# A forward pass on one core: the attention heads divide their outputs instead of their weights, and run in a fixed order on TensorE

## The chip, the core and the metric

The kernel runs on one core of a Trainium2 chip. The core has a matrix engine (TensorE, PE in the profile; its weight loads are listed apart as PEld), VectorE (DVE), ScalarE (ACT), GpSimd (POOL) and SyncE (SP), which here issues the loads from memory. The engines share an on-chip memory (SBUF) and the accumulators that TensorE writes into (PSUM), and run side by side, joined by semaphores. The metric is the time of one execution in microseconds, as the median of several runs: 2803.64 us for the kernel before (three runs, 2803.21 to 2806.1).

## The reference, cut to what matters

A sequence of 512 positions with 1024 features goes through two layers with four mixing branches each ("mix") and two feed-forward blocks, then a recurrent block, an MLP, a banded attention with 16 heads, and another MLP. Two places have heads: the latent attention of each mix (8 heads), and the banded attention. Both end in a softmax and a product with the values:

```python
# in each mix, per block of 128 queries q0:kend, for 8 heads
s = (einsum('bqhd,bkhd->bhqk', q_nope[:, q0:kend], k_nope[:, :kend])
     + einsum('bqhr,bkr->bhqk', q_rope[:, q0:kend], k_rope[:, :kend])) * scale
p = jax.nn.softmax(where(mask, s, NEG_INF), axis=-1)
outs.append(einsum('bhqk,bkhd->bqhd', p, v[:, :kend]))

# in the banded attention, per chunk of 64 queries, for 16 heads
sc = einsum('bqhd,bhkd->bhqk', qb, kb) * scale + bias
p = jax.nn.softmax(where(valid, sc, -inf), axis=-1)
o = einsum('bhqk,bhkd->bqhd', p, vb)
```

A softmax is an exponential divided by the sum of its row. The division can be done on the weights p, or, since the product is linear, on the rows of the output.

## The kernel before

All of it is float32. Activations lie transposed, as 8 tiles of 128 features by 512 positions. A large product is done as three matmuls of a shorter format (`mm3`, L149 to L153): high x high, high x low and low x high parts. The parts are made by `split` (L104): ScalarE copies the high part (L109), VectorE or GpSimd subtracts it for the low part (L110). `load` (L123) fetches weights and splits them; a gain is multiplied in on GpSimd (L138).

`heads` (L332) runs both kinds of heads. A head has four blocks of 128 queries, with 128, 256, 384 and 512 keys. `scores` (L270) makes a block's scores in one of two banks "s": TensorE's products (L279, or `mm3` in a mix), VectorE's row maximum (L291, or L295 with the bias), ScalarE's exponential with the row's sum beside it (L292, L297), VectorE's reciprocal of the sum (L298), and the scaling of the weights (L302 on VectorE for the first three blocks, L300 on ScalarE for the last). Two blocks later, `turn` (L305) transposes the scaled block on TensorE (L314) into one of two banks "t" and splits it into `pth` and `ptl`; after the fourth block, eight matmuls with the values follow (L325, "the products") into the only bank "o". ScalarE copies one half of that bank (L329), and `done` adds the other half to it on VectorE (L523 in a mix, L1030 in the attention).

In the attention a head's keys and queries come from `doubled` (L945): VectorE makes a tile `two` (L949), TensorE transposes it in four pieces (L953) into a bank "t". `stacked` (L957) splits the keys (`kh`, `kl`), and makes the queries `q` on ScalarE (L963) and VectorE (L965). All that is the step `prep`, done while the head before is at its second block.

What fills TensorE between the pieces of a head is `filler` (L1036): the projections of the next four heads' queries, keys and values (`quarter`, 256-wide matmuls), and then the first products of the attention's output. `heads` takes 96 such steps, spread evenly. A mix takes 68 steps of its other branches. The list `marks`, used in the attention alone, makes a step of the filler wait in the program's order for the turn before it. Everything else in the order of each engine is set by a scheduler, which takes instructions by priority when what they need is there by its own reckoning; the pieces of a head have a higher priority (`hi`) than the rest.

Of the kernel before, what the change touches and what calls it, by code (L numbers as in the profile page):

```python
# [18 lines left out]
P = 128  # L19
# [47 lines left out]
class Net:  # L67
    def __init__(self, ctx, tc, d, out):
# [6 lines left out]
        self.half = self.small.tile([P, 32], F32, name="half")  # L75
# [194 lines left out]
    def scores(self, it, qb):  # L270
# [5 lines left out]
        if rows is None:  # L276

            for a, n in zip(k, range(2)):
                nc.tensor.matmul(out=s[:, :w], lhsT=q[:, qs], rhs=a[:, :w], start=n == 0, stop=n == 1)  # L279
        else:  # L280
            self.mm3(s[:, :w], (q[0][rows, qs], q[1][rows, qs]), (k[0][rows, :w], k[1][rows, :w]), True, True)
# [7 lines left out]
        sm = self.t(self.small, "sm", 6, (P, 1))  # L289
# [8 lines left out]
        nc.vector.reciprocal(out=sm, in_=sm)  # L298
        if qb == 3:
            nc.scalar.activation(out=p, in_=p, func=AF.Copy, scale=sm)  # L300
        else:
            nc.vector.tensor_scalar(out=p[:, :w], in0=p[:, :w], scalar1=sm, scalar2=None, op0=ALU.mult)  # L302
        return p

    def turn(self, it, qb, p):  # L305
# [13 lines left out]
        if qb == 3:  # L319

            o = self.ps("o")
            for kb in range(4):
                bs = slice(4 * kb, 4 * kb + 4 - kb)
                for pt in (pth, ptl):
                    nc.tensor.matmul(out=o[:, kb * P:], lhsT=it["v"](kb), rhs=pt[:, bs],  # L325
                                     start=kb == 0 and pt is pth, stop=kb == 3 and pt is ptl)
# [3 lines left out]
            it["done"](o[a], f[a], a)  # L330

    def heads(self, items, filler, total, marks=None, hi=1000, depth=2):  # L332


        pend = []
        places, place, given = 8 * len(items) + 2 * depth, 0, 0

        def turn():
            with self.tc.high_priority(offset=hi):
                self.turn(*pend.pop(0))  # L340
            if marks is not None:
                marks.append(self.mark.ins)

        def fill():
            nonlocal place, given
            place += 1
            while given * places < total * place:
                given += 1
                with self.tc.issue_after(marks[-1]) if marks else ExitStack():
                    next(filler, None)  # L350

        items[0]["prep"](items[0])
        for n, it in enumerate(items):
            for qb in range(4):
                with self.tc.high_priority(offset=hi):
                    pend.append((it, qb, self.scores(it, qb)))
                fill()
                if len(pend) > depth:
                    turn()
                if qb == 1 and n + 1 < len(items):  # L360
                    items[n + 1]["prep"](items[n + 1])
                fill()
        while pend:
            fill()
            turn()
# [5 lines left out]
    def mix(self, l, gnext):  # L371
# [10 lines left out]
        with tc.tile_pool(name=f"att{l}", bufs=1, reuse_waits="tile") as ap:  # L382
# [136 lines left out]
            def item(hd):  # L519
                j = hd // 2  # L520

                def done(o, f, rows):
# [689 lines left out]
```

## Time and profile before

| | kernel before |
|---|---|
| median of 3 runs | 2803.64 us (2803.21 to 2806.1) |
| the profiled execution | 2796.84 us |
| its span, mean granted clock of TensorE | 2795.1 us, 0.991 |
| TensorE busy | 2719.6 us, 97%, 13616 matmuls |
| VectorE busy | 1570.9 us, 56% |
| ScalarE busy | 1148.8 us, 41% |
| GpSimd busy | 443.4 us, 16% |

The profiled execution is a run of its own; its span runs from the first to the last instruction. Busy times of different engines overlap, so they do not add up to the span. A granted clock of 1 is TensorE's higher level (2.4 GHz), 0.5 the lower (1.2 GHz). By the timeline, the first mix's heads run from about 78 to 199 us, the second's from about 890 to 1014, and the attention's from about 2196 to 2429.

### The profile page before, as it was taken

What the parts mean: (1) busy time and instruction counts of PE and PEld (TensorE: products, weight loads), DVE (VectorE), ACT (ScalarE), POOL (GpSimd) and SP (SyncE); (2) the same over time, 40 slices, a digit from 0 to 9 for tenths busy, and PEclk for the clock granted to TensorE, in tenths of its full rate; (3) what the DMA queues carried; (4) which work ended last, traced back from release to release, by engine and by line L of the source; (5) the groups of instructions that cost most, each with busy time, mean ns of one, the idle gap of its engine ahead of it and who ended that gap; (6) DMA issues with size and microseconds to landing.
All of it is one profiled execution on the core that took longest, in us unless ns stands there. A gap on an engine that the chain in (4) does not pass through costs nothing.

```text
span 2795.1 us, 34599 instructions
## 1 busy us (share of the span) xinstructions
PE 2719.6 (97%) x13616; PEld 2304.5 (82%) x13616; DVE 1570.9 (56%) x2420; ACT 1148.8 (41%) x1894; POOL 443.4 (16%) x350
## 2 busy tenths in 40 slices
PE   8999999999999999999999998999999999899999
PEld 7778889888898778888888886888888888788887
DVE  5875555534467865456344478744444688744443
ACT  5553234322255543234222358433323567533222
POOL 5401110100004211101000100100004674200000
PEclk9999999999999999999999999999999999999999
DMA  4213232233322123242333322233223211133322
GB/s 152 63 46 98 92 106 89 91 100 96 96 89 95 48 64 98 93 132 64 95 96 100 92 93 78 77 106 97 94 96 97 72 63 63 63 98 92 105 95 87
DMA packets 77348, 249.70 MB, mean 89 GB/s; under 512 B 8577, under 2 KB 14593, under 8 KB 77185
## 3 DMA queue, kind: packets, MB, share of 16 engines
q1 hardware_dynamic: 77184, 247.49, 27.7%
q8 instruction: 107, 1.75, 0.3%
q14 instruction: 57, 0.46, 0.1%
HBM read 245.36 MB, written 2.10 MB: 89 GB/s over the span
## 4 chain that ended last, share of the span: by engine, by line
PE 88%; DVE 7%; ACT 3%; issue 1%; DMA 0%; POOL 0%; SPq 0%; DVEq 0%; ACTq 0%
PE ps_mm L151 16%; PE ps_mm L152 16%; PE ps_mm L153 16%; PE ps_s L152 9%; PE ps_s L151 9%; PE ps_s L153 9%; PE ps_o L153 3%; PE ps_o L152 3%; PE ps_o L151 3%; PE ps_o L325 1%; PE ps_t L314 1%; PE ps_s L279 1%; DVE xl L237 1%; ACT wh L109 1%; DVE S L214 0%
## 5 line engine op out<-in xcount | busy, mean ns | idle before, releaser
L109 ACT ACTIVATE wh<-raw 128x1024 fp32r<-128x1024 f32 (+3 forms) x403 | 411.8, 1024 | 1178.8 <-PE ps_mm L152 458.0
L110 DVE TENSOR_TENSOR wl<-raw,wh 128x1024 fp32r<-128x1024 f32 (+3 forms) x403 | 514.8, 1279 | 164.8 <-ACT wh L109 155.0
L151 PE MATMUL ps_mm<-xh,wh 128*128 128x512 f32 x1160 | 453.8, 392 | 7.3 <-ACT xh L112 6.8
L152 PE MATMUL ps_mm<-xl,wh 128*128 128x512 f32 x1160 | 453.2, 391 | 0.5 <-DVE xl L113 0.5
L153 PE MATMUL ps_mm<-xh,wl 128*128 128x512 f32 x1160 | 452.7, 391 | 0.0
L151 PEld LDWEIGHTS ps_mm<-xh,wh 128*128 128x128 f32 x1160 | 218.4, 188 | 53.8 <-ACT xh L112 6.8
L152 PEld LDWEIGHTS ps_mm<-xl,wh 128*128 128x128 f32 x1160 | 218.5, 188 | 45.4 <-DVE xl L113 1.0
L153 PEld LDWEIGHTS ps_mm<-xh,wl 128*128 128x128 f32 x1160 | 218.3, 188 | 45.4
L153 PE MATMUL ps_s<-xh,wl 128*128 128x512 f32 x552 | 215.5, 390 | 0.0
L151 PE MATMUL ps_s<-xh,wh 128*128 128x512 f32 x552 | 215.1, 390 | 0.0
L152 PE MATMUL ps_s<-xl,wh 128*128 128x512 f32 x552 | 214.8, 389 | 0.0
L151 PE MATMUL ps_mm<-hh,wh 128*128 128x512 f32 (+1 forms) x422 | 161.2, 382 | 0.0
L152 PE MATMUL ps_mm<-hl,wh 128*128 128x512 f32 (+1 forms) x422 | 160.9, 382 | 0.0
L153 PE MATMUL ps_mm<-hh,wl 128*128 128x512 f32 (+1 forms) x422 | 160.9, 382 | 0.0
L690 POOL TENSOR_TENSOR a<-a,rb 128x512 f32<-128x512 f32 x44 | 60.2, 1371 | 534.2 <-DVE a L689 534.2
L624 POOL TENSOR_TENSOR m<-m,g 128x512 f32<-128x512 f32 x48 | 62.6, 1304 | 433.4 <-DVE g L623 433.3
L153 PEld LDWEIGHTS ps_s<-xh,wl 128*128 128x128 f32 x552 | 103.6, 188 | 22.3 <-DVE wl L110 0.9
L151 PEld LDWEIGHTS ps_s<-xh,wh 128*128 128x128 f32 x552 | 103.7, 188 | 21.4
L152 PEld LDWEIGHTS ps_s<-xl,wh 128*128 128x128 f32 x552 | 103.6, 188 | 21.4
L151 PE MATMUL ps_s<-hh,wh 128*128 128x512 f32 (+1 forms) x308 | 117.0, 380 | 0.0
L152 PE MATMUL ps_s<-hl,wh 128*128 128x512 f32 (+1 forms) x308 | 116.8, 379 | 0.0
L153 PE MATMUL ps_s<-hh,wl 128*128 128x512 f32 (+1 forms) x308 | 116.8, 379 | 0.0
(462 smaller groups left out, 5858.4 us busy)
## 6 DMA issues: line engine op xcount, KB each, us to landing
raw<-in_w_in SPq DMA_DIRECT2D x96, 512.0 KB, 3.5
raw<-in_w_gu SPq DMA_DIRECT2D x88, 512.0 KB, 3.5
raw<-in_w_down SPq DMA_DIRECT2D x80, 512.0 KB, 3.5
raw<-in_w_up SPq DMA_DIRECT2D x64, 512.0 KB, 3.5
raw<-in_w_down SPq DMA_DIRECT2D x32, 448.0 KB, 3.3
raw<-in_w_qkv SPq DMA_DIRECT2D x24, 512.0 KB, 3.4
raw<-in_w_out SPq DMA_DIRECT2D x16, 512.0 KB, 3.5
raw<-in_a_w_in SPq DMA_DIRECT2D x16, 512.0 KB, 3.6
```

The source lines that it names most:

```text
L109: a = nc.scalar.activation(out=h, in_=src, func=AF.Copy)
L110: b = (eng or nc.vector).tensor_tensor(out=l, in0=src, in1=h.bitcast(F32), op=ALU.subtract)
L151: mm(out=ps, lhsT=a[0], rhs=b[0], start=first, stop=False)
L152: mm(out=ps, lhsT=a[0], rhs=b[1], start=False, stop=False)
L153: self.multiplied = mm(out=ps, lhsT=a[1], rhs=b[0], start=False, stop=last)
L237: lambda: self.nc.vector.scalar_tensor_tensor(out=l, in0=x, scalar=g, in1=h.bitcast(F32), op0=ALU.mult, op1=ALU.subtract))
L279: nc.tensor.matmul(out=s[:, :w], lhsT=q[:, qs], rhs=a[:, :w], start=n == 0, stop=n == 1)
L314: self.mark = nc.tensor.transpose(out=pt[:, ks], in_=p[:, ks], identity=self.c("ident"))
L325: nc.tensor.matmul(out=o[:, kb * P:], lhsT=it["v"](kb), rhs=pt[:, bs], start=kb == 0 and pt is pth, stop=kb == 3 and pt is ptl)
L624: G.tensor_tensor(out=m, in0=m, in1=g, op=ALU.add)
L690: G.tensor_tensor(out=a, in0=a, in1=rb, op=ALU.mult)
```

## The change

The scaling of the weights and the reciprocals of single blocks go. The sums of a head's four blocks stand in one tile of four columns. After the products, VectorE takes one reciprocal of the four, TensorE spreads them over the partitions by four transposes (`spread`, L203) into a bank "t", and `done` gets a multiplication by that bank behind the addition. This holds for mixes and attention.

In the attention every piece is now tied to the one before (`behind`), so that TensorE's order there is written out and not left to the scheduler. The products follow a step of filler later than the last turn; keys' and queries' transposes go into the bank "o" in place of "t", and they and their tiles `two` are made at other places in the sequence, up to two heads ahead (`plan`). The filler has 88 steps in a pace of its own; the values of the first four heads (`lead`) are made between the first heads' transposes, and the keys of the second four before the heads. The widening of `half` has no use in these stages.

```diff
 def scores(self, it, qb):
...
-        sm = self.t(self.small, "sm", 6, (P, 1))
+        if qb == 0:
+            it["sm"] = self.t(self.small, "sm", 2, (P, 4))
+        sm = it["sm"][:, qb:qb + 1]
...
-        nc.vector.reciprocal(out=sm, in_=sm)
-        if qb == 3:
-            nc.scalar.activation(out=p, in_=p, func=AF.Copy, scale=sm)
-        else:
-            nc.vector.tensor_scalar(out=p[:, :w], in0=p[:, :w], scalar1=sm, scalar2=None, op0=ALU.mult)
         return p
...
 def turn(self, it, qb, p):
...
-        if qb == 3:
+        def products():
             o = self.ps("o")
...
             nc.scalar.activation(out=f[a], in_=o[b], func=AF.Copy)
-            it["done"](o[a], f[a], a)
+            nc.vector.reciprocal(out=it["sm"], in_=it["sm"])
+            with self.tc.issue_after(end.ins):
+                over = self.spread(it["sm"], range(4))
+            it["done"](o[a], f[a], over[a], a)
+        return products if qb == 3 else None
...
 def heads(...):
...
         for n, it in enumerate(items):
             for qb in range(4):
-                with self.tc.high_priority(offset=hi):
+                with self.tc.high_priority(offset=hi), behind():
                     pend.append((it, qb, self.scores(it, qb)))
+                if marks is not None:
+                    marks.append(self.scored.ins)
                 fill()
+                products()
                 if len(pend) > depth:
                     turn()
-                if qb == 1 and n + 1 < len(items):
-                    items[n + 1]["prep"](items[n + 1])
+                for at, far, what in plan:
+                    if qb == at and n + far < len(items):
+                        with behind():
+                            items[n + far][what](items[n + far])
+                        if marks:
+                            marks.append(self.flipped.ins)
                 fill()
...
 def attention(self, gnext):
...
-                ps = self.ps("t")
+                return two
+
+            def turned(two):
+                ps = self.ps("o")
...
-                def done(o, f, rows):
+                def done(o, f, over, rows):
...
                     V.tensor_tensor(out=f, in0=o, in1=f, op=ALU.add)
+                    V.tensor_tensor(out=f, in0=over, in1=f, op=ALU.mult)
                     self.split((os_[j][0][rows], os_[j][1][rows]), f, eng=G)
...
-            self.heads([item(hd) for hd in range(16)], filler(), 96, [])
+            lead = part(0, 1)
+            next(lead), next(lead)
+            self.heads([item(hd) for hd in range(16)], filler(), 88, [],
+                       plan=((2, 2, "first"), (3, 2, "second"), (0, 1, "third")),
+                       pace=lambda n: max(min(0.71 * n, 14.1 + 0.53 * n), n - 46), lead=lead)
```

`first` makes `two` of the keys, `second` transposes and splits the keys and makes `two` of the queries, `third` transposes and converts the queries and fetches the bias.

In TensorE's program the eighth head of the attention ended so before: the last products of `pth` and `ptl` with the values `v`, the next queries' transposes (L953, into a bank `ps_t`), one transpose of the next head's first weights (L314), then filler.

```order
L325 MATMUL ps_o_18924<-pth_18796,v_18278 128x128
L325 MATMUL ps_o_18924<-ptl_18797,v_18278 128x128
L953 MATMUL ps_t_18954<-tab,two_18952 128x128 [waits DVE_49,PE_49]
L953 MATMUL ps_t_18954<-tab,two_18952 128x128 x3
L314 MATMUL ps_t_19008<-tab,p_18871 128x128 [waits DVE_49,PE_49]
L151 MATMUL ps_mm_18845<-wh_18987,xh_16981 128x256
L152 MATMUL ps_mm_18845<-wl_18988,xh_16981 128x256
L153 MATMUL ps_mm_18845<-wh_18987,xl_16982 128x256
```

And so now, with new line numbers: L322 for the products, L203 for the spread of the sums `sm`, L311 for transposes of weights, L1000 for the keys' transposes into the outputs' bank `ps_o`.

```order
L322 MATMUL ps_o_19186<-pth_19015,v_18072 128x128
L322 MATMUL ps_o_19186<-ptl_19016,v_18072 128x128
L203 MATMUL ps_t_19198<-tab,sm_18878 128x128 x4
L311 MATMUL ps_t_19209<-tab,p_19082 128x128 [waits PE_49]
L311 MATMUL ps_t_19246<-tab,p_19119 128x128 [waits DVE_49]
L311 MATMUL ps_t_19246<-tab,p_19119 128x128
L1000 MATMUL ps_o_19253<-tab,two_19213 128x128 [waits Activation_49]
L1000 MATMUL ps_o_19253<-tab,two_19213 128x128 x3
L151 MATMUL ps_mm_19157<-wh_19160,xh_16839 128x256
L152 MATMUL ps_mm_19157<-wl_19161,xh_16839 128x256
L153 MATMUL ps_mm_19157<-wh_19160,xl_16840 128x256
```

The transposes of the first and second block now follow the products and the spread at once, and the keys' transposes come behind them; before, a step of filler stood between the two blocks' transposes.

On VectorE, around the same head's addition, it was so before: the keys' low half, `two` (L949), the addition (L1030), the queries (L965), the low half of the next head's first block, and the maxima (L295).

```order
L110 TENSOR_TENSOR kl_19148<-ps_t_19151,kh_19147 128x512 [waits Activation_49]
L949 TENSOR_TENSOR two_19343<-qr_18831,fac_18830 128x512 [waits PE_49]
L1030 TENSOR_TENSOR of_19142<-ps_o_19133,of_19142 64x512 [waits Activation_49]
L965 SCALAR_TENSOR_TENSOR q_19158<-ps_t_19161,rv_17084,q_19158 64x512 [waits Activation_49]
L110 TENSOR_TENSOR ptl_19206<-ps_t_19207,pth_19205 128x128 [waits Activation_49]
L295 ISA p_19262,mx_19261<-ps_s_19258,bias_3130_17087 128x128 [waits PE_49]
L295 ISA mx_19261 128x1
```

Now the one reciprocal (L328) and the addition (L1082) stand ahead of the next head's first low half, and the multiplication by the spread sums (L1083) behind it.

```order
L328 RECIPROCAL sm_19083<-sm_19083 128x4 [waits Activation_49]
L1082 TENSOR_TENSOR of_19195<-ps_o_19186,of_19195 64x512 [waits Activation_49]
L110 TENSOR_TENSOR ptl_19208<-ps_t_19209,pth_19207 128x128 [waits Activation_49]
L1083 TENSOR_TENSOR of_19195<-ps_t_19198,of_19195 64x512 [waits DVE_49]
L992 TENSOR_TENSOR two_19393<-qr_18344,fac_18343 128x512 [waits PE_49]
L110 TENSOR_TENSOR ptl_19208<-ps_t_19246,pth_19207 128x2x128 [waits Activation_49]
L110 TENSOR_TENSOR kl_19252<-ps_o_19253,kh_19251 128x512 [waits Activation_49]
L297 ISA p_19278,mx_19277<-ps_s_19274,bias_3098_17023 128x128 [waits PE_49,Pool_49]
```

The scalings and the single reciprocals are gone from the queue, and the first block's low half stands behind the addition.

At the end of the attention TensorE went, before, from the last products straight to matmuls that read the last head's output (`kh_20388`, `kl_20389`).

```order
L325 MATMUL ps_o_20491<-pth_20411,v_19935 128x128
L325 MATMUL ps_o_20491<-ptl_20412,v_19935 128x128
L151 MATMUL ps_mm_20515<-kh_20388,wh_20510 128x512 [waits Activation_49]
L151 MATMUL ps_mm_20528<-kh_20388,wh_20510 128x512
L151 MATMUL ps_mm_20543<-kh_20388,wh_20510 128x512
L152 MATMUL ps_mm_20515<-kl_20389,wh_20510 128x512 [waits Pool_49]
```

Now the spread and fifteen matmuls that read earlier heads' outputs stand ahead of those that read the last one (`kh_20257`).

```order
L322 MATMUL ps_o_20348<-ptl_20264,v_19742 128x128
L203 MATMUL ps_t_20360<-tab,sm_20182 128x128 [waits PE_49]
L203 MATMUL ps_t_20360<-tab,sm_20182 128x128 x3
L151 MATMUL ps_mm_20370<-oh_19381,wh_20313 128x512
L152 MATMUL ps_mm_20370<-ol_19382,wh_20313 128x512
L153 MATMUL ps_mm_20370<-oh_19381,wl_20314 128x512
L151 MATMUL ps_mm_20370<-oh_19721,wh_20313 128x512
...
L153 MATMUL ps_mm_20415<-kh_20001,wl_20383 128x512
L151 MATMUL ps_mm_20387<-kh_20257,wh_20382 128x512 [waits Activation_49]
L151 MATMUL ps_mm_20400<-kh_20257,wh_20382 128x512
```

These fifteen stood ahead of the last products before, or later in the output's product.

## Rows read from the trace of the kernel before

**Rows 1.** The page: busy time of the engines (first part), and the chain that ended last.

```profile
PE 2719.6 (97%) x13616; PEld 2304.5 (82%) x13616; DVE 1570.9 (56%) x2420; ACT 1148.8 (41%) x1894; POOL 443.4 (16%) x350
...
PE 88%; DVE 7%; ACT 3%; issue 1%; DMA 0%; POOL 0%; SPq 0%; DVEq 0%; ACTq 0%
```

**Rows 2.** Table by stretch: busy us (instructions) of PE, PEld, DVE, ACT, POOL; clock; DMA.

```profile
75.00:200.00 125.00, 116.06 (x587) 96.75 (x585) 95.15 (x217) 66.30 (x152) 29.35 (x22) 0.96 0.19 59
...
890.00:1015.00 125.00, 114.27 (x584) 94.06 (x582) 96.34 (x218) 67.08 (x156) 28.09 (x21) 0.98 0.19 59
...
2190.00:2430.00 240.00, 218.57 (x1553) 202.59 (x1551) 199.12 (x457) 159.11 (x360) 109.96 (x80) 0.98 0.20 66
```

**Rows 3.** Waits of TensorE, 2190 to 2430 us: us in total, times, longest us.

```profile
PE ps_t L314 <- DVE q L965: 7.5, 7, 2.7
PE ps_t L314 <- DVE kl L110: 4.9, 6, 1.4
```

**Rows 4.** Timeline, start of the attention's heads: start us, us, engine, line [idle before].

```profile
2195.48 0.60 PE L953 MATMUL ps_t<-tab,two 128*128 128x128 f32 x4
2195.83 0.31 PE L279 MATMUL ps_s<-kh,q 128*128 128x128 f32 x1
...
2202.95 0.48 PE L279 MATMUL ps_s<-kh,q 128*128 128x128 f32 x1 [4.67 <-DVE q L965]
...
2203.74 2.59 DVE L302 TENSOR_SCALAR p<-p,sm 128x128 f32<-128x128 f32 x3
...
2204.21 1.90 POOL L138 TENSOR_TENSOR raw<-raw,prm 128x1024 f32<-128x1024 f32 x1 [3.73 <-DMA raw<-in_w_qkv]
...
2206.52 0.28 DVE L110 TENSOR_TENSOR ptl<-ps_t,pth 128x128 fp32r<-128x128 f32 x1
```

**Rows 5.** Table by stretch: the 7 us behind the wait at the start.

```profile
2201.00:2208.00 7.00, 5.01 (x22) 4.82 (x23) 6.13 (x19) 2.91 (x8) 3.05 (x3) 0.52 0.28 96
```

**Rows 6.** Groups of VectorE, 2190 to 2430 us: count, busy us, mean ns, idle before.

```profile
L302 DVE TENSOR_SCALAR p<-p,sm 128x128 f32<-128x128 f32 (+2 forms) x48 | 27.2, 575 | 0.9
...
L1030 DVE TENSOR_TENSOR of<-ps_o,of 64x512 f32<-64x512 f32 x16 | 11.0, 685 | 4.1 <-ACT of L329 4.0
...
L298 DVE RECIPROCAL sm<-sm 128x1 f32<-128x1 f32 x64 | 9.8, 155 | 2.9 <-ACT p L297 2.9
```

**Rows 7.** The scalings L302 alone, 2190 to 2430 us: duration ns, min/median/max.

```profile
L302 DVE TENSOR_SCALAR p<-p,sm x48: 264/378/2127, 2203.7 to 2417.1; 128x128 f32<-128x128 f32 x16, 128x256 f32<-128x256 f32 x16, 128x384 f32<-128x384 f32 x16
```

**Rows 8.** Timeline, end of the attention's heads.

```profile
2423.64 0.39 PE L152 MATMUL ps_mm<-ol,wh 128*128 128x512 f32 x1
2423.87 0.40 PE L153 MATMUL ps_mm<-oh,wl 128*128 128x512 f32 x1
...
2428.71 0.28 PE L325 MATMUL ps_o<-ptl,v 128*128 128x128 f32 x1
...
2429.70 0.69 DVE L1030 TENSOR_TENSOR of<-ps_o,of 64x512 f32<-64x512 f32 x1 [2.02 <-ACT of L329]
...
2431.11 0.97 PE L151 MATMUL ps_mm<-kh,wh 128*128 128x512 f32 x3 [2.12 <-ACT kh L109]
```

**Rows 9.** Timeline, last products, copy and addition of two heads.

```profile
2317.57 0.28 PE L325 MATMUL ps_o<-ptl,v 128*128 128x128 f32 x1
...
2319.08 0.69 DVE L1030 TENSOR_TENSOR of<-ps_o,of 64x512 f32<-64x512 f32 x1
...
2330.24 0.28 PE L325 MATMUL ps_o<-ptl,v 128*128 128x128 f32 x1
...
2333.56 0.60 ACT L329 ACTIVATE of<-ps_o 64x512 f32<-64x512 f32 x1
2334.25 0.67 DVE L1030 TENSOR_TENSOR of<-ps_o,of 64x512 f32<-64x512 f32 x1
```

**Rows 10.** Waits of TensorE, first mix's heads, 75 to 200 us.

```profile
PE ps_mm L151 <- DVE sm L298: 1.6, 1, 1.6
```

**Rows 11.** Waits of TensorE, second mix's heads, 890 to 1015 us.

```profile
PE ps_t L314 <- DVE p L302: 1.3, 1, 1.3
```

More of the change, by code (lines that the diff above doesn't have):

```diff
@@ L73, in __init__ @@
         self.prm = self.small.tile([P, NPRM], F32, name="prm")
[L75 removed]
+        self.half = self.small.tile([P, 64], F32, name="half")
         self.nc.gpsimd.memset(self.half[:, :16], -0.5)
@@ L278, in scores @@
             for a, n in zip(k, range(2)):
-                nc.tensor.matmul(out=s[:, :w], lhsT=q[:, qs], rhs=a[:, :w], start=n == 0, stop=n == 1)
+                self.scored = nc.tensor.matmul(out=s[:, :w], lhsT=q[:, qs], rhs=a[:, :w], start=n == 0, stop=n == 1)
         else:
@@ L324, in turn @@
                 for pt in (pth, ptl):
-                    nc.tensor.matmul(out=o[:, kb * P:], lhsT=it["v"](kb), rhs=pt[:, bs],
-                                     start=kb == 0 and pt is pth, stop=kb == 3 and pt is ptl)
+                    end = nc.tensor.matmul(out=o[:, kb * P:], lhsT=it["v"](kb), rhs=pt[:, bs],
+                                           start=kb == 0 and pt is pth, stop=kb == 3 and pt is ptl)
             a, b = (slice(0, 64), slice(64, 128))[::it["step"]]
@@ L520, in item @@
                 j = hd // 2
-                def done(o, f, rows):
-                    V.tensor_tensor(out=aout[j][rows], in0=o, in1=f, op=ALU.add)
+                def done(o, f, over, rows):
+                    V.tensor_tensor(out=f, in0=o, in1=f, op=ALU.add)
+                    V.tensor_tensor(out=aout[j][rows], in0=over, in1=f, op=ALU.mult)
                     if hd in (0, 2, 4):
@@ L1010, in out, with first, second, third @@
                         self.norm_step(n, i, ALL)
-            groups = [[] for _ in range(4)]
+            groups = [[None] * 3 for _ in range(4)]
             def item(hd):
                 group, h = groups[hd // 4], hd % 4
-                def prep(it):
-                    stacked(it, group[0][0], group[1][0], h)
+                def first(it):
+                    it["two"] = doubled(group[0], h)
+                def second(it):
+                    stacked_keys(it)
+                    it["two"] = doubled(group[2], h)
+                def third(it):
+                    stacked_queries(it)
                     b = bias[hd % 2]
@@ L1024, in prep, with done @@
                     it["bias"] = b
-                def done(o, f, rows):
+                def done(o, f, over, rows):
                     j = hd // 2
```

107 lines of the change are left out of this document (66 added, 41 removed).

## The prediction

> **What bounds the kernel now.** I read the first part of the page, then the chain that ended last. TensorE works in 97% of the span, and 88% of the chain is its own work, against 7% for VectorE and 3% for ScalarE [rows 1]. So the time is TensorE's work plus its idle time, and another engine counts only where TensorE waits for it. The table by stretch shows where that is: the two mixes' heads (75 to 200 and 890 to 1015 us) and the attention's (2190 to 2430 us) leave TensorE idle for 8.9, 10.7 and 21.4 us, and VectorE is busy for 95, 96 and 199 us there [rows 2]. That is 41 of the span's 75 idle us, in the only three stretches that the change touches.
>
> The waits of the attention say whom TensorE waits for: VectorE's half of the query split seven times (7.5 us), its low half of the keys six times (4.9 us), and one wait of 4.7 us at the first head [rows 3]. All sit where a bank of transposes must be read out before the next may be written. The timeline shows the one at the start: the second head's first scores, at 2202.95, stood 4.67 us behind the query split, which VectorE reached late [rows 4]. After that pause the granted clock was 0.52 for 7 us [rows 5]; that is the lower of the two levels, 1.2 GHz.
>
> **The change part by part, on the profiled execution (2796.84 us; span 2795.1).** The median of the runs shown is 2803.64, so 6.8 us are added at the end.
>
> *1. Spread of the sums.* Each head gets four more transposes. Four in a row go from 2195.48 to the next matmul's start at 2195.83, which is 0.35 us [rows 4]. 16 heads cost 5.6 us and each mix's 8 cost 2.8, on TensorE, which nothing covers: +11.2 us in all.
>
> *2. VectorE's and ScalarE's work.* In the attention 48 scalings (27.2 us) and 64 reciprocals (9.8 us) go [rows 6], 37.0 us. What comes is a multiplication of 64x512 per head, which I price as the addition of the same shape, 0.685 us [rows 6], and one reciprocal of four columns, priced as the one of one column, 0.155: 16 x 0.84 = 13.4 us. VectorE is left with 23.6 us less of 199. ScalarE loses 16 scalings. A mix has half as many heads, so about half of each. None of it is on the path by itself. Its worth is only that what TensorE waits for comes sooner.
>
> Here the trace and a rule of the Trainium skill meet. The 48 scalings took 0.264 us at the least, 0.378 in the median and 2.127 at the most [rows 7]; a burst of three of them took 2.59 us, from 2203.74 to 2206.33, while GpSimd's multiplication ran from 2204.21 to 2206.11 [rows 4]. The Trainium skill, SBUF — State Buffer, section "Who interferes with whom", says that a VectorE operation using two ports and a GpSimd operation exclude each other, and that the later one stands still until the first is through. The trace agrees with that. By the rule the part of the 27.2 us above 48 x 0.378 = 18.1 was standing still, and 9.1 us of it may fall to the next VectorE operation with two inputs in SBUF, so that the relief would be 14.5 us instead of 23.6; item 4 would then move half of the way to its upper value, and the sum be 4 to 5 us higher.
>
> *3. Start and end of the attention.* After the change, 24 matmuls of other work stand between the queries' transposes and the scores that need them, and the second head's keys are made before the heads start. I let the 4.67 us go [rows 4], and of the slow clock behind it the 48% lost in 5.01 busy us [rows 5], 2.4 us: -7.1, and -4.7 if the clock falls for another reason. At the end TensorE finished the last products at 2428.99 (2428.71 + 0.28) and stood till 2431.11 for the copy, the add and the high half [rows 8]: 2.1 us. Now fifteen 512-wide matmuls stand between, 0.23 us each as 2423.64 to 2423.87 shows, 3.5 us, against a chain that grows by one multiplication of 0.69: 2.12 + 0.69 = 2.8. I take -2.1, and -1.4 if the multiplication is late by as much again.
>
> *4. The turns.* This is the new wait. After the products TensorE does the four spread transposes and one transpose of the next head's first block. The second block's transposes need a bank that is free only when VectorE has taken the low half of the first block, and VectorE has the output's addition ahead of that in its queue, which itself waits for ScalarE's copy. Behind the waiting addition stand the block's low half, the multiplication and the next keys' split; behind the waiting transposes stand the keys' transposes and the next scores. How long is the way from the last product to the end of the addition? The shortest is at the end of the attention, 2428.99 to 2430.39, 1.40 us [rows 8]; at 2317.85 it ended 1.92 us later, and at 2330.52, 4.40 us later [rows 9]. The split of a first block adds 0.28 [rows 4] and hand-overs about 0.1; the spread and the one transpose cover 0.45. With nothing else between, TensorE waits 1.40 + 0.38 - 0.45 = 1.3 us at the least and 1.9 at the middle one. In the order of the changed program eight of the 15 heads have nothing between, one has two matmuls, five have eight or nine (about 1 us, if a 256-wide one takes half of the 0.23), and one has twenty. At the least this is 9 x 1.3 + 5 x 0.3 = 13 us; at the middle 9 x 1.9 + 5 x 0.9 = 22 us; by a way of 2.5 us, 9 x 2.4 + 5 x 1.4 = 29. Keys and queries share the outputs' single bank, so the queries' transposes wait for the keys' low half: 0 to 1 us a head, of which I take 0.2, 3 us. What goes is the idle time that is not the start's or the end's: 21.4 - 4.7 - 1.0 (2428.99 to 2430) = 15.7 us. So 22 + 3 - 15.7 = +9, between -3 (13 and nothing for the bank) and +16 (29 and 3). I take the middle way because VectorE's queue gets shorter but ScalarE's copy keeps its place behind exponentials.
>
> Attention: 5.6 - 7.1 - 2.1 + 9 = +5; ends 5.6 - 7.1 - 2.1 - 3 = -7 and 5.6 - 4.7 - 1.4 + 16 = +16.
>
> *5. The mixes.* The spread costs 2.8 each. The waits for the reciprocal (1.6 us in the first) and for a scaled block (1.3 us in the second) go by themselves [rows 10, 11]. Of the rest of the 8.9 and 10.7 us, VectorE's 12 us of relief may take some; against that the last three turns of each mix now follow one another on two banks, one of which is read by the multiplication: some 0.7 us, as long as that is. I take +2 each, with ends -4 (two thirds of the idle time gone) and +6 (nothing gone, and the new wait twice more).
>
> The sum is 5 + 4 = +9: 2806 on the profiled execution, 2812 on the median.
>
> **The rivals.** *Faster: the relief reaches the waits.* The turn's way stays at 1.40 us because VectorE, 24 us lighter, is idle when the copy ends; the slow clock is gone; the mixes lose half of their idle time. Attention -7, mixes -2 each: 2793. For it: VectorE is 83% busy there and its scalings stand right among the waits. Against it: the shortest way was seen where nothing else was queued.
>
> *No change.* The 11.2 us of spread are what the start, the end and some reciprocal waits give back, 7.1 + 2.1 + 2.9 = 12.1, and the turns' waits only change their name: 2803.
>
> *Slower by much: the outputs' bank decides.* One bank now carries products, keys and queries. If ScalarE's copy is late by what it was at 2330.52 (3.04 us from the products' end to the copy's start at 2333.56 [rows 9]) in every second head, keys' transposes, and with them the turns, wait 2.5 us a head on average: 29 + 5 - 15.7 = +18 in place of +9, and a stretch at half clock, as in [rows 5], adds 2 to 3. It decides from the point where the way is longer than about 2.4 us. That gives 2803.6 + 9 + 9 + 2.4 = 2824. For it: the fixed order leaves TensorE nothing to go on with, while each piece of other work now has its place.
>
> *The change doesn't do what it says.* The order is fixed in the program and the scalings are gone, so only the separation of products and turns could fail; it does where nothing stands between, and that is in the sum.
>
> **How the numbers follow.** Forecast (slower by some 9 us) 0.36, faster rival 0.31, no change 0.21, bank rival 0.12. A measurement of this kernel can tell 0.2%, 5.6 us, from no change. The forecast lies 3 us beyond that, so about a fifth of its chance falls within: slower 0.29 + 0.12 = 0.41, and 0.02 more from no change, 0.43; same 0.07 + 0.17 = 0.24; faster 0.31 + 0.02 = 0.33. The ends of the items added up would be 2803.6 - 7 - 8 = 2789 and 2803.6 + 16 + 12 = 2832; the range that leaves out a fifth goes from 2791 to 2826. As both signs hold much of it, the forecast's own range is 2805 to 2819.
>
> **What would show it.** In the profile after: TensorE's busy time up by about 11 us; VectorE in the attention near 176 us; the wait of 4.7 us at the first head gone, and the 2.1 us at the last head's end gone; in their place 13 to 30 us of waits of the turn's transposes for VectorE's low half of a block, once a head. If these waits stay under 10 us, or the mixes lose over 5 us of idle time each, the forecast is wrong on the fast side. If TensorE waits for the keys' low half more than 10 us, the bank decides.

## The result, and the profile after

The changed kernel takes 2816.16 us (median of 6 runs, 2814.08 to 2817.15) against 2800.35 us of the kernel before, run beside it: a ratio of 1.0061 with an interval of 1.005 to 1.0072, slower by some 16 us. The profiled execution has a span of 2814.0 us, 18.9 more than before; the profile of before is of a run below its median (2796.84 us), the one after of a run at its median (2815.83).

The page's first part and its chain, to be read beside [rows 1]:

```profile
PE 2736.8 (97%) x13744; PEld 2320.2 (82%) x13744; DVE 1538.7 (55%) x2260; ACT 1128.7 (40%) x1862; POOL 442.4 (16%) x350
...
PE 88%; DVE 7%; ACT 3%; issue 1%; POOL 1%; DMA 0%; ACTq 0%; DVEq 0%
```

TensorE is busy for 17 us more, and VectorE and ScalarE for 32 and 20 us less; the chain is TensorE's as before. Where the time came in is read most exactly from the starts of the same matmul in both traces, counted from the program's start, with the matmuls that were added left out:

| same matmul | start before | start after | gained so far |
|---|---|---|---|
| ahead of the first mix's heads | 70.13 | 70.36 | +0.2 |
| feed-forward behind it | 250.03 | 251.90 | +1.9 |
| ahead of the second mix's heads | 870.05 | 872.05 | +2.0 |
| recurrent block behind it | 1300.18 | 1308.44 | +8.3 |
| MLP ahead of the attention | 2100.18 | 2108.45 | +8.3 |
| MLP behind the attention | 2600.02 | 2618.93 | +18.9 |

So the first mix costs 1.6 us, the second 6.3, the attention 10.6, and the rest of the program next to nothing. The stretches of the heads, in the columns of [rows 2]:

```profile
75.00:202.00 127.00, 118.32 (x621) 97.63 (x619) 87.60 (x178) 61.50 (x146) 30.67 (x22) 0.99 0.18 58
890.00:1020.00 130.00, 120.77 (x621) 99.96 (x620) 90.00 (x179) 61.20 (x147) 31.50 (x22) 0.97 0.18 58
2190.00:2452.00 262.00, 235.29 (x1689) 219.61 (x1687) 187.13 (x379) 154.92 (x350) 116.05 (x84) 0.97 0.19 60
```

The attention's heads end some 18 us later, so its stretch is longer here. In it TensorE is idle for 26.7 us; before, it was idle for 21.4 us in [rows 2] and 1.8 more from 2430 to 2452. The waits of the same stretch, in the columns of [rows 3]:

```profile
PE ps_t L311 <- DVE ptl L110: 19.8, 12, 4.4
PE ps_o L1000 <- DVE kl L110: 3.9, 4, 3.4
PE ps_o L322 <- DVE ptl L110: 1.6, 2, 0.8
PE ps_o L1000 <- DVE sm L328: 0.8, 1, 0.8
```

The transposes of weights no longer wait for the query split or the keys' low half [rows 3], and the first head's 4.67 us [rows 4] are gone too. In their place 12 waits of the transposes of weights (L311) for the low half of a block make 19.8 us. This is one of them, head eight, from the last product on, with start, length, engine, line and the idle time ahead in brackets:

```profile
2342.11 0.28 PE L322 MATMUL ps_o<-ptl,v 128*128 128x128 f32 x1
2342.22 0.62 PE L203 MATMUL ps_t<-tab,sm 128*128 128x128 f32 x4
...
2342.49 0.59 ACT L326 ACTIVATE of<-ps_o 64x512 f32<-64x512 f32 x1 [0.57 <-PE ps_o L322]
...
2342.68 0.27 PE L311 MATMUL ps_t<-tab,p 128*128 128x128 f32 x1
...
2343.10 0.28 ACT L109 ACTIVATE pth<-ps_t 128x128 fp32r<-128x128 f32 x1
2343.11 0.70 DVE L1082 TENSOR_TENSOR of<-ps_o,of 64x512 f32<-64x512 f32 x1 [0.98 <-ACT of L326]
...
2343.83 0.29 DVE L110 TENSOR_TENSOR ptl<-ps_t,pth 128x128 fp32r<-128x128 f32 x1
...
2344.16 0.69 DVE L1083 TENSOR_TENSOR of<-ps_t,of 64x512 f32<-64x512 f32 x1
2344.18 0.44 PE L311 MATMUL ps_t<-tab,p 128*128 128x128 f32 x2 [1.23 <-DVE ptl L110]
...
2344.46 0.60 PE L1000 MATMUL ps_o<-tab,two 128*128 128x128 f32 x4
```

The products end at 2342.39, ScalarE copies at once, VectorE adds, and only then takes the low half of the first block, till 2344.12; TensorE goes on at 2344.18. From the last product to the addition's end it is 1.42 us, nearly the shortest way of [rows 8], and TensorE stands for 1.23 us. The longest wait, 4.37 us, is the second head's:

```profile
2246.84 0.27 PE L322 MATMUL ps_o<-ptl,v 128*128 128x128 f32 x1
...
2248.57 1.77 POOL L144 TENSOR_TENSOR wl<-raw,wh 128x512 fp32r<-128x512 f32 x1 [1.32 <-ACT wh L141]
2249.13 2.36 DVE L110 TENSOR_TENSOR v<-sq,v 128x256 fp32r<-128x256 f32 x3
...
2249.29 0.72 ACT L299 ACTIVATE p<-p,mx 128x512 f32<-128x512 f32 x1
...
2250.43 0.59 ACT L326 ACTIVATE of<-ps_o 64x512 f32<-64x512 f32 x1
...
2251.93 0.69 DVE L1082 TENSOR_TENSOR of<-ps_o,of 64x512 f32<-64x512 f32 x1
...
2252.65 0.29 DVE L110 TENSOR_TENSOR ptl<-ps_t,pth 128x128 fp32r<-128x128 f32 x1
...
2253.00 0.69 PE L311 MATMUL ps_t<-tab,p 128*128 128x128 f32 x2 [4.37 <-DVE ptl L110]
```

Here ScalarE's copy came 3.3 us after the products (ended 2247.11), behind splits, an exponential and its sum, and the addition another 0.9 us after the copy, since splits of values stood ahead. Three of these took 2.36 us, of which GpSimd's split ran beside the first 1.2, till 2250.34. With this wait the clock fell to its lower level, and stayed there till 2258:

```profile
2252.00:2258.00 6.00, 5.00 (x24) 5.00 (x25) 4.82 (x8) 1.61 (x3) 3.51 (x2) 0.50 0.18 74
```

It fell twice more in the attention, for about half as long, with waits of 3.36 us (at 2318) and 3.18 us (at 2360).

At the end of the attention's heads, where [rows 8] has 2.12 us of idle time, TensorE now runs from the last product to the matmuls that need it with no gap, and waits only 0.61 us for GpSimd's half:

```profile
2446.65 0.27 PE L322 MATMUL ps_o<-ptl,v 128*128 128x128 f32 x1
...
2448.44 0.69 DVE L1083 TENSOR_TENSOR of<-ps_t,of 64x512 f32<-64x512 f32 x1
...
2450.71 0.86 PE L151 MATMUL ps_mm<-kh,wh 128*128 128x512 f32 x3
...
2452.18 0.50 PE L152 MATMUL ps_mm<-kl,wh 128*128 128x512 f32 x1 [0.61 <-POOL kl L110]
```

The multiplication and the reciprocal, whose prices were taken from others, in the columns of [rows 6]:

```profile
L1083 DVE TENSOR_TENSOR of<-ps_t,of 64x512 f32<-64x512 f32 x16 | 11.0, 684 | 0.3
...
L328 DVE RECIPROCAL sm<-sm 128x4 f32<-128x4 f32 x16 | 2.7, 171 | 4.8 <-ACT p L299 4.7
```

And in the first mix two waits that [rows 10] did not have, for a bank t; the second mix has the same two with the same numbers:

```profile
PE ps_t L311 <- DVE ptl L110: 2.3, 2, 2.0
...
PE ps_t L311 <- DVE aout L566: 0.8, 2, 0.5
```

### The profile page after: what moved, and what is told of

It reads as the page before. It is cut to its first block, busy times and chain, and to the rows that moved or that the text cites. A ratio compares the mean times of both kernels' runs of the same rounds, so it can differ in the third digit from the quotient of the medians.

```text
span 2814.0 us, 34711 instructions
## 1 busy us (share of the span) xinstructions
PE 2736.8 (97%) x13744; PEld 2320.2 (82%) x13744; DVE 1538.7 (55%) x2260; ACT 1128.7 (40%) x1862; POOL 442.4 (16%) x350
## 4 chain that ended last, share of the span: by engine, by line
PE 88%; DVE 7%; ACT 3%; issue 1%; POOL 1%; DMA 0%; ACTq 0%; DVEq 0%
PE ps_mm L151 16%; PE ps_mm L152 16%; PE ps_mm L153 16%; PE ps_s L153 9%; PE ps_s L152 9%; PE ps_s L151 9%; PE ps_o L153 3%; PE ps_o L152 3%; PE ps_o L151 3%; PE ps_o L322 1%; PE ps_t L311 1%; DVE xl L237 1%; DVE wl L110 1%; PE ps_o L1000 1%; DVE ptl L110 1%
```

## The experiments

All ran with five rounds beside the kernel before, whose median was 2797.8 to 2799.0 us on these chips. The table gives, from one profile of each run, by how many us a stage is longer than in the profile of before, by the same matmuls as in the table above: the first mix from 70.13 to 250.03, the second from 870.05 to 1300.18, the attention from 2100.18 to 2600.02. The last two columns are of the attention: TensorE's idle time, and the time lost to the lower clock (busy time multiplied by what is lacking to a clock of 1).

| run | first mix | second mix | attention | idle | lost to the clock |
|---|---|---|---|---|---|
| kernel before | | | | 23.2 | 4.3 |
| changed kernel | +1.6 | +6.3 | +10.6 | 26.9 | 5.9 |
| 1 sums spread in a bank mm | +1.2 | +6.1 | -0.9 | 18.1 | 3.3 |
| 2 new order, old division | -0.8 | -1.2 | +11.2 | 30.9 | 9.9 |
| 3 old order, new division | +1.1 | +6.1 | +43.4 | 44.0 | 21.5 |
| 4 keys and queries in t again | +2.2 | +6.3 | +22.2 | 29.9 | 12.9 |
| 5 keys later | +2.0 | +5.3 | +0.2 | 18.9 | 2.7 |
| 6 keys later, weights scaled | 0.0 | -1.2 | +1.3 | 24.9 | 5.1 |
| 7 division in the attention alone | +0.5 | -1.0 | +2.1 | 19.2 | 4.9 |
| 8 the mixes' sums in mm too | +2.8 | +2.9 | -2.5 | 16.5 | 3.4 |
| 9 the best parts together | -0.1 | -0.1 | -0.4 | 17.0 | 5.1 |
| 10 keys and queries in mm | -1.0 | -0.3 | +8.8 | 25.8 | 5.4 |
| 11 no division at all | -9.7 | -6.6 | +0.8 | 24.6 | 6.2 |
| 12 mixes without multiplication | -8.0 | -2.8 | +11.2 | 26.1 | 7.7 |

The attention with the same edits came out up to 2.1 us apart in three profiles (runs 1, 8 and 9), a mix with the same edits up to 1.5, so differences of that size are not read as any. The stretch between the second mix and the attention, which no edit touches, differs by -1.6 to +2.2 us; the expectations that call the attention of run 1 "2 us under that of the kernel before" have it counted in. A profile can also lie under its run's median (2804.83 against 2809.21 us in run 5), so stages and medians do not add up exactly.

**Where the sums are spread.** Only the bank is another, in the attention:

```diff
-                over = self.spread(it["sm"], range(4))
+                over = self.spread(it["sm"], range(4), it.get("over", "t"))   # "mm" for the attention's heads
```

> The changed kernel with one difference: in the attention the sums are spread into one of the three banks of the projections (mm) and not into one of the two banks t. Theory (the second block's transposes wait for a bank t that is free only behind the addition, 19.8 us in 12 waits): these waits fall under 6 us; the keys' transposes, which stand behind them and need the outputs' bank, then wait for copy and addition themselves (0.6 + 0.7 us against 0.7 us of transposes, some 0.7 us in 8 to 11 heads, 6 to 8 us), so the time falls by 8 to 14 us against the changed kernel, to 2802 to 2808. Rival (the outputs' bank decides, the wait only changes its name): the keys' transposes take over all of it, within 4 us of the changed kernel. Rival (the pace of the fixed order costs the time): no change, within 3 us.

Measured: 2804.94 us, ratio 1.0024 (1.0015 to 1.0033); the attention is 11.5 us shorter than in the changed kernel. The turns' waits for a bank t are gone, and the keys' transposes wait instead:

```profile
PE ps_o L1000 <- DVE of L1082: 10.8, 8, 3.2
PE ps_o L1000 <- DVE kl L110: 4.1, 5, 2.5
```

The time fell by what the theory had, so the wait of the turns was more than a name: it was the bank. But what stands next in TensorE's order still waits for the same addition (`of`): 10.8 us in 8 waits, where the theory had 6 to 8.

**The new order with the old division.** Weights scaled again in `scores`, block by block as before, and no spread or multiplication:

```diff
-            nc.vector.reciprocal(out=it["sm"], in_=it["sm"])
-            with self.tc.issue_after(end.ins):
-                over = self.spread(it["sm"], range(4))
-            it["done"](o[a], f[a], over[a], a)
+            it["done"](o[a], f[a], None, a)
...
```

> The changed kernel's order, plan, pace and banks, but the weights are scaled block by block as before, without spread and multiplication, in mixes and attention. Theory (spread and turn's wait cost the time, the order gains at start and end): the mixes are as before the change (8 us less than after), the attention loses 5.6 us of spread and most of the 19.8 us of waits for the low half, while VectorE has 24 us more to do: 2792 to 2802 in all, attention 3 to 10 us under that of the kernel before. Rival (the fixed order costs the time): attention still 5 to 10 us over that of before, 2805 to 2812.

Measured: 2806.42 us, ratio 1.0033 (1.0021 to 1.0046); attention +11.2.

```profile
PE ps_o L1000 <- DVE of L1082: 20.2, 11, 4.5
PE ps_o L1000 <- DVE kl L110: 6.5, 4, 4.2
```

The theory was right on the mixes and wrong on the attention: with no spread at all it costs as much as in the changed kernel, and the time is in the rival's range. With the banks t free, the keys' transposes into the outputs' bank wait 20.2 us for the addition. So a loss comes without the new division too: the fixed order puts something that needs a bank right behind the products, whichever it is.

**The old order with the new division.** The kernel before, with the `scores`, `turn` and `done` of the changed one; order, keys and queries as before.

> The kernel before with the division alone: outputs divided by the sums in mixes and attention, by four transposes into a bank t and a multiplication, order left to the scheduler, keys and queries through banks t as before. Theory: the mixes as after the change (8 us over before), the attention 5.6 us of spread over before, less up to 6 us of VectorE's relief, plus waits for banks t that the spread now also takes (0 to 8): 2807 to 2817. Rival (the order costs the time, the division is worth its price): attention under that of before by 0 to 5, 2802 to 2807.

Measured: 2848.74 us, ratio 1.0184 (1.017 to 1.0198); attention +43.4.

```profile
PE ps_t L954 <- DVE of L1032: 15.0, 8, 2.4
PE ps_t L954 <- DVE kl L110: 9.6, 4, 2.8
PE ps_t L954 <- DVE rs_v L184: 8.3, 2, 4.6
PE ps_t L311 <- DVE kl L110: 5.8, 2, 3.2
```

Both readings missed: the division by itself costs the attention 43 us, with keys and queries, spread and turns all in two banks t. Of these, 20.8 us are idle time, 17.2 are lost to the lower clock, which came twelve times there, and 5.4 are more work of TensorE. The fixed order takes 33 of them back. (`rs_v` is in the norm of the next heads' queries; L954 is here the keys' and queries' transposes.)

**Keys and queries in the banks t again**, in the changed kernel:

```diff
             def turned(two):
-                ps = self.ps("o")
+                ps = self.ps("t")
```

> The changed kernel with the keys' and queries' transposes put back into the banks t. Theory (the turn's wait for the low half behind the addition decides): the waits only grow, as three kinds of transposes share two banks: 2814 to 2830. Rival (the outputs' single bank decides): the waits of the keys' transposes (3.9 us and what hides behind them) go, faster by 4 us or more, under 2812.

Measured: 2829.09 us, ratio 1.0109 (1.0095 to 1.0123); attention +22.2.

```profile
PE ps_t L311 <- DVE ptl L110: 23.6, 15, 3.2
```

As the theory had it: the same waits, in 15 places in place of 12. But they are only 3.8 of the 11.6 us by which the attention is longer than in the changed kernel, and idle time grew by 3.0 us in all; 7.0 us are lost to the lower clock. Against the banks t, the single bank "o" was no loss.

**Keys later.** The first run's kernel with the keys' transposes two blocks away from the products:

```diff
-                       plan=((2, 2, "first"), (3, 2, "second"), (0, 1, "third")),
+                       plan=((2, 2, "first"), (0, 1, "second"), (1, 1, "third")),
```

> The run with the spread in a bank mm, with one more difference: keys' transposes at the first block of the head after (not two blocks after the products), queries' transposes one block later. Theory (whatever stands behind the addition of the output in TensorE's order waits for it; the first run left 10.8 us of such waits on the keys' transposes): these fall under 3 us, the attention is 8 to 12 us shorter than in the first run, which was 2 us under that of the kernel before; in all 2793 to 2797 against 2798 of before. Rival (the single bank is always late, whoever takes it): the waits move to the queries' transposes or the products, within 4 us of the first run.

Measured: 2809.21 us, ratio 1.0037 (1.0023 to 1.0051); attention +0.2, against -0.9 in the first run.

```profile
PE ps_o L1000 <- DVE kl L110: 7.6, 10, 3.4
PE ps_o L322 <- DVE q L1016: 5.0, 6, 1.5
PE ps_t L311 <- DVE ptl L110: 4.8, 3, 3.0
```

The waits for the addition are gone, but 17.4 us of others are there: among them the products now wait for the queries' split, which has the bank. The rival's account of it held, though by the medians it is 4.3 us from the first run.

**Keys later, weights scaled**: the second run's kernel with the plan just shown.

> The same new places of keys and queries, with the weights scaled block by block as before the change, no spread (the second run with the keys later). Theory: there the keys' transposes waited 20.2 us for the addition and 6.5 for the keys' low half; both go, the attention falls from 11 us over that of before to 5 to 12 us under it, in all 2784 to 2792. If the division on the outputs is itself worth something in this order (VectorE 24 us lighter), its attention is over that of the run with the keys later and the spread, although 5.6 us of spread are saved. Rival (scaling makes VectorE the bound in the fixed order): still over that of before.

Measured: 2800.82 us, ratio 1.0012 (1.0003 to 1.0021); attention +1.3, against +11.2 with the keys early. The theory failed, as it had the attention 5 to 12 us under that of before; the rival's outcome came.

```profile
PE ps_t L314 <- DVE ptl L110: 10.9, 5, 4.0
```

Here no spread takes a bank t and no keys stand behind the products, and the turns wait for the low half behind the addition all the same. In the longest of these waits VectorE's addition ended at 2309.82, the low half at 2310.14, and TensorE went on at 2310.29. With this plan, scaling and division (+0.2 and +2.1 in two profiles) cost the attention about the same.

**Division in the attention alone**, with the later keys:

```diff
         scores: per block
-        sm = it["sm"][:, qb:qb + 1]
+        if "over" not in it:                      # the mixes' heads
+            sm = self.t(self.small, "sm", 6, (P, 1))
...
+        if "over" not in it:                      # reciprocal and scaling as before the change
+            nc.vector.reciprocal(out=sm, in_=sm)
...
+            if "over" not in it:
+                it["done"](o[a], f[a], None, a)   # no spread, no multiplication
```

> Division on the outputs in the attention alone, sums spread into a bank mm, keys and queries at the later places; the mixes scale their weights as before the change. Theory: the mixes give back the 7 to 8 us that they lost (2.8 us of spread each, and waits), the attention is that of the run with the keys later: 2785 to 2790, faster than both kernels. Rival (the mixes' loss is the clock alone): 2791 to 2796.

Measured: 2799.0 us, ratio 1.0 (0.9991 to 1.0009); attention +2.1. Both ranges were missed: the mixes came out as the theory had them, the attention did not gain.

**The mixes' sums in a bank mm too**, on the first run's kernel:

```diff
-                return dict(hd=hd, step=1 - hd % 2 * 2, rows=ALLP, ...)
+                return dict(over="mm", hd=hd, step=1 - hd % 2 * 2, rows=ALLP, ...)
```

> The first run (spread in a bank mm in the attention, keys as in the changed kernel) with the mixes' sums also spread into a bank mm. Theory (the last turns of a mix wait 2.1 us for a bank t that the spread has taken, in each mix): these waits go, each mix is 1.5 to 3 us shorter, in all 2798 to 2802 against 2804.9 of the first run. Rival (the four transposes themselves and the slower clock at the end of the mix are the loss): within 2 us of the first run.

Measured: 2800.95 us, ratio 1.001 (1.0001 to 1.0019). The whole is in the range, but not by the theory: against the first run the first mix is 1.6 us longer and the second 3.2 shorter. Without the time lost to the lower clock (6.5 and 4.7 us here, 3.2 and 7.2 there) they are 1.7 and 0.6 us shorter, and TensorE's idle time in them is what it was (10.5 and 11.4 us against 10.3 and 11.6). That is inconclusive on the waits for the bank.

**The best parts together**: the first run's kernel with the mixes' edit of the division in the attention alone.

> The first run's attention (spread in a bank mm, keys as in the changed kernel, 2 to 4 us under that of the kernel before in two profiles), and mixes that scale their weights as before the change. Theory (the mixes' division costs 7 to 8 us, the attention's pays once its sums leave the banks t): 2794 to 2797 against 2798 of before. Rival (what the stages gain apart is lost in the clock): 2797 to 2801.

Measured: 2797.07 us, ratio 0.9993 (0.9984 to 1.0002); attention -0.4. This is on the edge of both ranges, some 0.7% faster than the changed kernel by the two ratios, and not to be told from the kernel before.

**Keys and queries in the banks mm**, on the run just told:

```diff
             def turned(two):
-                ps = self.ps("o")
+                ps = self.ps("mm")
```

> The run before this one with the keys' and queries' transposes in the banks mm too, so that nothing but the products uses the outputs' bank. Theory (what stands behind the outputs' addition waits only as long as it needs the same bank): the waits of the keys' transposes for the addition (10.8 us in the first run) and for the keys' low half (4.1) go, and the projections wait a little for the third bank (0 to 8 us): attention 5 to 15 us shorter, 2782 to 2792. Rival (the three banks mm become the tight place, since each pair of projections holds two until ScalarE has read them): waits of the projections of 10 us and more, 2797 to 2810.

Measured: 2809.8 us, ratio 1.0042 (1.0028 to 1.0056); attention +8.8.

```profile
PE ps_mm L1011 <- DVE of L1094: 14.6, 7, 4.4
PE ps_mm L151 <- DVE of L1094: 3.3, 1, 3.3
```

The theory of that run failed: with a bank apart from the outputs the keys' transposes wait longer, 14.6 us, because the bank they get is the one that the spread has taken, and `of` at L1094 is the multiplication behind the addition. The time is in the rival's range, but its mechanism is not what came: the projections waited once, 3.3 us.

**No division at all**, in the changed order: the second run's kernel without its scaling.

```diff
-        nc.vector.reciprocal(out=sm, in_=sm)
-        if qb == 3:
-            nc.scalar.activation(out=p, in_=p, func=AF.Copy, scale=sm)
-        else:
-            nc.vector.tensor_scalar(out=p[:, :w], in0=p[:, :w], scalar1=sm, ...)
         return p
```

> The changed kernel's order and banks with the division left out altogether: neither scaled weights nor spread sums, so the outputs of all heads lack the division by the sums. It prices the order with the lightest VectorE and with no spread. Theory (in the changed kernel 5.6 us are spread and 12 to 13 us the wait for the bank t, and what is left waits for the addition as in the first run): attention 6 to 11 us under that of before; mixes 2.8 us and the last turns' waits under the changed kernel's, 0 to 3 us under those of before; in all 2785 to 2793. Rival (the fixed order itself costs, as the 11 us of the run with scaled weights seemed to say): attention at or over that of before, 2797 or more.

Measured: 2779.19 us, ratio 0.9932 (0.9919 to 0.9946); mixes -9.7 and -6.6, attention +0.8.

```profile
PE ps_o L995 <- DVE of L1077: 17.7, 12, 3.3
PE ps_o L995 <- DVE kl L110: 4.6, 2, 3.9
```

Even with the lightest VectorE and no spread, the attention in the fixed order is no shorter than before, as the rival had it: 17.7 us of waits for the addition. Still it is 10.4 us shorter than with scaled weights in the same order (run 2). The time is under both ranges, for both missed the mixes: in the scheduler's order they gain by the lighter engines the whole 16.3 us by which this span is shorter than that of before.

**The mixes without the multiplication**, on the changed kernel:

```diff
-                    V.tensor_tensor(out=f, in0=o, in1=f, op=ALU.add)
-                    V.tensor_tensor(out=aout[j][rows], in0=over, in1=f, op=ALU.mult)
+                    V.tensor_tensor(out=aout[j][rows], in0=o, in1=f, op=ALU.add)
```

> The changed kernel with the mixes' sums still inverted and spread, but the mixes' outputs not multiplied by them: the mixes' outputs lack the division, the attention is as in the changed kernel. It tells what took back the 9.7 and 6.6 us that the mixes gained on those of before with no division at all. If it is the multiplication (on VectorE ahead of the next low halves, and as the last reader of a bank t): the mixes come out at 7 and 4 us under those of before, 2.8 us of spread apart from the run without division, in all 2796 to 2802. If it is the spread on TensorE and its bank: the mixes stay at 1 and 5 us over those of before, 2812 to 2817.

Measured: 2800.33 us, ratio 1.0007 (0.9998 to 1.0016); mixes -8.0 and -2.8 (against +1.6 and +6.3 with the multiplication). The first reading held, roughly, in both. The multiplication, with the wait for the bank that it reads, is worth 9.6 and 9.1 us in the two mixes. Of that, 4.3 and 2.7 us are time at the lower clock; the rest, 5.3 and 6.4, is near the length of eight multiplications, 5.5 us. How it is shared between VectorE's queue and the bank is not shown, but moving the sums to a bank mm (run 8) left the idle time as it was.

## Why the prediction was right, point by point

The forecast was slower by 9 us to 2812; measured was 16 us slower at 2816, inside the range. The way, the place and the kind of the waits came as forecast, the size was a little more than half. That 2816 is so near to 2812 is in part luck: the forecast was added to 2803.64, the median of three runs of the kernel before, while three later runs of it took 2797.4 to 2797.5 and the median of all six is 2800.35. Step by step:

1. *The spread.* TensorE is busy for 17 us more, 11.2 of them forecast. Of the rest, 3.1 us is time at the lower clock, half of it between the second mix and the attention, which the change does not touch. Without that, TensorE's busy time grew by 5.2 and 3.5 us in the mixes and 5.4 in the attention, forecast 2.8, 2.8 and 5.6; why the first mix has more was not told apart.

2. *VectorE and ScalarE.* VectorE lost 32 us in all (1570.9 to 1538.7), of them 15.5 in the attention; the forecast was 23.6 there and two halves of it, 47 together. The multiplication cost its 0.684 us, the reciprocal 0.171. Of the splits of values, though, 16 took 12.0 us where they had taken 7.2 before, the long ones beside GpSimd's. By the Trainium skill's rule on the ports (SBUF — State Buffer, "Who interferes with whom") a VectorE instruction with two SBUF inputs contends with a GpSimd instruction that reads SBUF. The values' splits are such, and the three in the long wait ended 1.1 us after GpSimd's. So the standing still could have passed to them when the scalings went, as the prediction said. But with the scalings put back in the new order they took 11.9 us too, so the new order is enough for it; in the old order without the scalings they took 10.0, so a part may pass on there. (In the prediction, half of the way to item 4's upper value is 3.5 us, not 4 to 5.)

3. *Start and end.* Both came as forecast: no wait at the first head, and 0.61 in place of 2.12 + 0.39 us at the end. The clock did not. The lower level left the start and came back with the wait of 4.37 us, for as long as in [rows 5], and the attention has two shorter stretches of it besides, where it had one; it loses 5.9 us to it, before 4.3. Item 3 counted a gain of 2.4 us; it became a loss of 1.6, and this 4.0 us is most of the 5.6 us by which the attention was forecast too low.

4. *The turns.* The named wait is the one that came: 19.8 us for low halves against 22 forecast for the middle way, and 4.7 us for keys and reciprocal against 3. It came where it was forecast: the eight heads with nothing between waited 13.9 us, 1.7 each (forecast 1.9), the five with eight or nine matmuls between 4.8 us (forecast 4.5), nearly all of it the long wait of 4.37. The way from the last product to the addition's end was 1.41 us or under in 8 of 16 heads and 2.03 us on the mean, the longest 5.51; forecast was 1.92. But the reason was too narrow. The bank t is where the wait lands, and the two runs with early keys and without any spread (2 and 11) show 22 to 27 us of waits on the keys' transposes when no bank t is short. What decides is that the next thing in a fixed order needs VectorE behind an addition that waits for ScalarE.

5. *The mixes.* Forecast +2 each, measured +1.6 and +6.3. The difference of the two is the clock (0.96 to 0.99 in the first, 0.98 to 0.97 in the second): the time lost to it went from 7.4 to 4.3 us in the first and from 4.3 to 7.4 in the second, so that without it they lose 4.7 and 3.2. The turns' waits for a bank t are 3.1 us in each, the forecast had 0.7. The mis-sized term is the multiplication: with it left out the mixes gain 8.0 and 2.8 us, and with no division 9.7 and 6.6. So the two mixes had some 16 us of relief in them; the spread took 5 to 6 of that back, and the multiplication, put at 0.7 us of waits, 19 us, about 7 of it through the clock.

The rivals: *faster* had no support, the waits did not stay at the shortest way. *No change* was wrong, as the turns' waits were larger than the old ones. *The outputs' bank decides* has against it that TensorE waited 3.9 us for the keys' low half, not 10, and that the run with the banks t again was 13 us slower, though its point, that the way to the addition decides and not its end, was near the cause.

What stays open: how the scheduler's order with the new division came to its waits and slow stretches (run 3; that order was not followed), how the multiplication's price in the mixes divides between queue and bank, and what scatters the attention by 2 us. An addition that comes earlier, by another place of ScalarE's copy, was not tried.

## What to carry to other kernels

Work taken off an engine that is not the bottleneck is worth what the waits for it were worth. In the same fixed order, leaving out scalings and reciprocals made the attention 10.4 us shorter (run 2 against run 11), and dividing on the outputs took 9.8 us of that back with the sums in a bank t, and none of it with the sums in a bank mm (run 1). Before a fixed order is written, ask of each step which bank or tile it needs and who reads that last. Moving the step that waits farther behind helped where it waited most (9.9 us, run 6 against run 2); where the bank had been changed already, it only moved the waits (run 5 against run 1). And an operation put into a queue ahead of what the bottleneck waits for is to be priced at the wait of those behind it and at the clock, not only at its own length: 5.5 us of multiplications cost a mix more than 9.

## What was not expected of the hardware

The clock's lower level came with waits and moved with them: with one of 4.67 us at 2202 before, with one of 4.37 us at 2253 after. It does not need a wait that long: in the first mix before it came at 88.4 behind a wait of 1.9 us, and in run 12 at 836.7 with no wait over 0.52 us just ahead. It made the same change cost 1.6 us in one mix and 6.3 us in the other, and in run 3 it cost nearly as much as the idle time that came with it, 17.2 us beside 20.8.
